# A head's outputs later in the queue of the matrix engine, and the last column's squares added up

## The chip, the cores and the metric

The kernel runs on one core of a Trainium2 chip. A core has a matrix engine (TensorE, PE in the profile, its weight loads PEld), two engines for elementwise work (VectorE, DVE; ScalarE, ACT), GpSimd (POOL) and SyncE (SP), which issues the transfers. Each engine takes its own instructions one after another, and waits where an instruction needs what another engine has not finished. The metric is the device time of one execution in microseconds.

## The reference

A trunk of two layers over 256 tokens of width 2048, in 32-bit floats. Each layer is a token mixer and a SwiGLU FFN, both behind an RMSNorm whose shift and scale come from a conditioning vector, and both added to x through a gate that comes from it too.

```python
for i in range(DEPTH):
    mod = (c_act @ w_mod[i] + b_mod[i])[:, None, :]
    sh1, sc1, g1, sh2, sc2, g2 = jnp.split(mod, 6, axis=-1)
    h = rms_norm(x, norm1_g[i]) * (1.0 + sc1) + sh1
    y = retention_mixer(h, ...) if i % 4 == 0 else short_conv_mixer(h, ...)
    x = x + g1 * y
    h = rms_norm(x, norm2_g[i]) * (1.0 + sc2) + sh2
    x = x + g2 * swiglu(h, ffn_w_in[i], ffn_w_out[i])
return rms_norm(x, final_g)
```

Layer 0 mixes by retention: eight heads, each with q and k (256 wide, rotated by position), v and a gate g (512 wide). A head's output is rms_norm(decayed causal scores of q and k, times v) times silu(g); all heads' outputs go through w_out. Layer 1 mixes by a gated convolution of width 3.

## The kernel before

**Products.** Every matrix product is made from two halves: each weight tile is rounded to a coarser format (hi, ScalarE, L413) and the rest is kept (lo, VectorE, L416), the activations likewise, and three products of halves are added up. TensorE multiplies blocks of 128 by 128. The weights lie in memory in the order of use, in chunks of 128 by 2048; a chunk makes two tiles of hi and lo, eight blocks each, and `take` hands the blocks out in order. `raw` has three buffers and hi and lo four each, so the preparation runs a few tiles ahead of TensorE. The conditioning vector's products are made on VectorE, one reduction (L327) for each of 192 chunks, spread over the kernel.

**Orders.** TensorE's order is that of the program. The order on VectorE, ScalarE and GpSimd outside the opening is made by a planner, which simulates the program with costs of its own and takes what is ready by priority. Accumulators are eight PSUM banks, given out in turn.

**Heads.** They run in the order 4, 0, 2, 1, 5, 3, 6, 7. The opening (`RET_SPANS`) computes parts of the heads 0 to 4 ahead, while the normed rows come one by one: head 4 has all 16 rows of q, k and its gate, heads 0 and 1 have 13 rows, heads 2 and 3 nine. What is made there is in `ahead`, under the head and the number of the bank: 0 for q, 1 for k, 2 and 3 for the two halves of the gate. `projections` does the rest of a head in this order: the rest of q and its rotation, the rest of k, v (16 rows of four blocks), the scores, and the rest of the gate. The head's outputs are not made there. `mixed` returns two pieces of work, `outputs` (nine matmuls of scores and v at L1055, a Square with its sum, a power on GpSimd, the product with the gate at L1064) and `turned` (eight transposes at L1074, and the split into halves), each with a number of blocks. They go to `asides`; `ticked` counts the blocks that the next work multiplies, and gives out the first piece when its number is reached, sets the count to 0, and then the second:

```python
since[0] += n
if asides and since[0] >= asides[0][0]:
    asides.pop(0)[1]()
    since[0] = 0
```

The numbers are `STEPS = (6, 26)`. The count goes up row by row: by two in q and k, by four in v, and by six in the first group of the output projection, which has six columns. That projection is done in two parts, after the fourth head (head 1) and after the eighth; a part's first group takes twelve of its sixteen rows for six columns, and then the last four rows for each of these, and all rows for each other column.

**Norms.** As a column of x is finished, `squares` adds its squares to `acc`: Square on ScalarE, addition on VectorE (L568). The first column, and before the change the last one too, goes into a tile of its own by a Square alone (L564). `norm_sums` then adds over partitions with matmuls against ones (L576), a set for each tile in the list. `normed` starts the next projection on rows that have only been scaled, does two rows, and has `norm_sums` after them; the power follows on GpSimd, and the spread of the result two rows later. `scaled_only` (L659, L660) makes each row as its column is done.

Of the kernel before, what the change touches and what calls it, by code (L numbers as in the profile page):

```python
# [48 lines left out]
STEPS = (6, 26)  # L49
# [69 lines left out]
def tiles_of(g):  # L119
    return sum(width for _, width in g.items) // P * len(g.ks)  # L120
# [147 lines left out]
def trunk(ctx: ExitStack, tc: tile.TileContext, x_in, c_in, pos_in, w_mod, cols_in, tab_in, w_all, out):  # L268
# [9 lines left out]
    def name(s):  # L278
        serial[0] += 1
        return f"{s}_{serial[0]}"  # L280

    def tmp(tag, shape=(P, S), dtype=F32, pool=work, bufs=None):
        return pool.tile(list(shape), dtype, tag=tag, name=name(tag), bufs=bufs)
# [8 lines left out]
    x = [x_all[:, j, :] for j in range(KT)]  # L292
# [52 lines left out]
    first = tiles_of(RET_SPANS[0])  # L345
# [16 lines left out]
    def needed(layer, which, last=KT - 1):  # L362
        while any(m[:2] == (layer, which) and m[2] <= last for m in todo):
            modulation(*todo.pop())
# [83 lines left out]
    def bank(tag=None):  # L448
        tag = tag or (lanes.pop(0) if lanes else lane[0])
        return ps[0].tile([P, 2, S], F32, tag=tag, name=name("bank"))  # L450
# [10 lines left out]
    def product(g, act, base=0, before=None, banks=None, last=True):  # L461

        fresh = not banks
        banks = banks or [bank() for _ in g.cols]
        if fresh and due_gap[0] <= 0:
            nc.tensor.transpose(banks[0][:, 0, :P], ident, ident)
            due_gap[0] = GAP_EVERY
        due_gap[0] -= len(g.cols) * len(g.ks)
        for k in g.ks:
            if before:  # L470
                before(k)
            h = act[k - base]
            for c, pt in zip(g.cols, banks):
                hi, lo = take(g, k, c)
                nc.tensor.matmul(  # L475
                    pt, hi, h, start=fresh and k == g.ks[0], stop=False, skip_group_check=True
                )
                nc.tensor.matmul(  # L478
                    pt[:, 1, :], lo, h[:, 0, :], start=False, stop=last and k == g.ks[-1], skip_group_check=True
                )  # L480
            ticked(len(g.cols))
        paced(len(g.cols) * len(g.ks))
        return banks

    def packed(g, act, base=0, before=None, between=None, banks=None):

        banks = banks or [bank() for _ in g.cols[::2]]
        for k in g.ks:
            if before:
                before(k)  # L490
            h = act[k - base]
            for i, c in enumerate(g.cols):
                if between and i == len(g.cols) // 2:
                    between(k)
                pt = banks[i // 2][:, i % 2, :]
                hi, lo = take(g, k, c)
                first, last = k == g.ks[0] and i % 2 == 0, k == g.ks[-1]
                nc.tensor.matmul(pt, hi, h[:, 0, :], start=first, stop=False, skip_group_check=True)  # L498
                nc.tensor.matmul(pt, hi, h[:, 1, :], start=False, stop=False, skip_group_check=True)  # L499
                nc.tensor.matmul(pt, lo, h[:, 0, :], start=False, stop=last, skip_group_check=True)  # L500
            ticked(len(g.cols))
        paced(len(g.cols) * len(g.ks))
        return banks

    def flat(pt):
        return pt.rearrange("p a b -> p (a b)")
# [54 lines left out]
    def squares(acc, t, tag="acc"):  # L561
        if acc is None:
            acc = tmp(tag, bufs=1)
            nc.scalar.activation(acc, t, AF.Square)  # L564
        else:
            sq = tmp("sq", bufs=2)
            nc.scalar.activation(sq, t, AF.Square)
            nc.vector.tensor_tensor(acc, acc, sq, op=ALU.add)  # L568
        return acc
# [142 lines left out]
    def output(groups, act, which, last, after=None, base=None):  # L712

        layer, gate = which[0], mod_g[which[0]][which[1] == GT2]
        first, *groups = groups
        due_gap[0] = 0
        base, acc = first.ks[0] if base is None else base, None
        banks = product(first, act, base, last=False)
        for j, g in enumerate(groups):
            needed(*which, j)  # L720
            col = gate[:, j : j + 1]
            if last and j == KT - 1:
                (pt,) = packed(g, act, base)
                nc.vector.scalar_tensor_tensor(x[j], pt[:, 0, :], col, x[j], op0=ALU.mult, op1=ALU.add)
                acc = [acc, squares(None, x[j], "acc1")]
                if after:
                    after(j)
                return acc
            (pt,) = product(g, act, base, banks=banks[j : j + 1])
            t = tmp("sum", bufs=4)  # L730
            nc.vector.scalar_tensor_tensor(t, pt[:, 1, :], col, x[j], op0=ALU.mult, op1=ALU.add)
            nc.vector.scalar_tensor_tensor(x[j], pt[:, 0, :], col, t, op0=ALU.mult, op1=ALU.add)
            if last:
                acc = squares(acc, x[j])
            if after:
                after(j)


    with ExitStack() as inner:
# [48 lines left out]
        ahead = {}  # L788
# [3 lines left out]
        def rm_pair(key, dtype=F32):  # L792
            tag_of[key] = free.pop(0)
            return rm.tile([P, 2, 2, S], dtype, tag=tag_of[key], name=name("rm"))
# [17 lines left out]
        with tc.tile_pool(name="start", bufs=1) as sp:  # L812
# [57 lines left out]
            with tc.manual_schedule(engines={mybir.EngineType.DVE, mybir.EngineType.Activation}):  # L870
# [24 lines left out]
                def square(i):  # L895

                    both = rm.tile([P, 2, 2, S], F32, tag=f"pair{i}", name=name("sq"))
                    sq = [both[:, n] for n in range(2)]
                    for n in range(2):
                        nc.scalar.activation(sq[n], x4[i][:, 2 * n : 2 * n + 2, :], AF.Square)  # L900
                    return sq
# [5 lines left out]
                acc = square(0)  # L907
# [136 lines left out]
        def mixed(head, both, v, sg):  # L1044

            total = tmp("rs", (P, 2), bufs=4)
            os = [rp.tile([P, DV], F32, tag="o", name=name("o"), bufs=2) for _ in range(2)]

            def outputs():
                pts = [bank() for _ in range(2)]  # L1050
                for t, pt in enumerate(pts):
                    for jt in range(t + 1):
                        a = both[jt][:, :, (t - jt) * P : (t - jt + 1) * P]
                        for x, y in ((0, 0), (0, 1), (1, 0)):
                            nc.tensor.matmul(  # L1055
                                flat(pt), a[:, x, :], v[:, jt, y, :], start=jt + x + y == 0, stop=jt == t and x == 1
                            )
                    nc.scalar.activation(os[t], flat(pt), AF.Square, accum_out=total[:, t : t + 1])
                r = tmp("rs", (P, 2), bufs=4)
                nc.vector.tensor_scalar(r, total, 1.0 / DV, EPS, op0=ALU.mult, op1=ALU.add)  # L1060
                root = tmp("rs", (P, 2), bufs=4)
                nc.gpsimd.tensor_tensor(root, r, half, op=ALU.pow)
                for t, pt in enumerate(pts):
                    nc.vector.scalar_tensor_tensor(  # L1064
                        os[t], flat(pt), root[:, t : t + 1], sg[t], op0=ALU.mult, op1=ALU.mult
                    )

            def turned():
                pts = [bank() for _ in range(2)]
                for i, pt in enumerate(pts):  # L1070
                    for j in range(2):
                        at = slice((2 * i + j) * P, (2 * i + j + 1) * P)
                        for t in range(2):
                            nc.tensor.transpose(pt[:, j, t * P : (t + 1) * P], os[t][:, at], ident)  # L1074
                for i, pt in enumerate(pts):
                    n = 2 * head + i
                    t = rm_pair(("mid", n), F32R)
                    nc.scalar.copy(t[:, :, 0, :], pt)
                    nc.vector.tensor_tensor(t[:, :, 1, :], pt, t[:, :, 0, :].bitcast(F32), op=ALU.subtract)
                    mid[2 * n], mid[2 * n + 1] = t[:, 0], t[:, 1]  # L1080

            return list(zip(STEPS, [outputs, turned]))

        def pair(head, i):

# [33 lines left out]
        acc = ret_out(1, True)  # L1119
# [29 lines left out]
    acc = swiglu(0, acc, lambda j: scaled_only(1, 0, j))  # L1149
# [4 lines left out]
    for i, g in enumerate(CONV_IN):  # L1154
        pending += [sums(g)] if i else normed(acc, 1, 0, g)
        while len(pending) >= 3:
            pb, pc, pu = pending[:3]
            pending = pending[3:]
            j = done
# [11 lines left out]
            split(mid[j], y)  # L1171
            done += 1
    acc = output(CONV_OUT, mid, (1, GT1), True, lambda j: scaled_only(1, 1, j))

    stage.close()
# [202 lines left out]
    acc = swiglu_tokens(1, acc, with_gain)  # L1378
# [48 lines left out]
```

## Time and profile before

| what | us |
|---|---|
| median of three runs | 2607.35 (2607.01 to 2611.01) |
| profiled execution | 2605.66 |
| span of its instructions | 2603.9 |
| TensorE busy in the span | 2571.1 |
| VectorE busy | 2178.4 |
| ScalarE busy | 1300.3 |

The granted clock of TensorE is 0.998 of full speed over the span. The profile lists groups of instructions by line of the program; "L1055" is line 1055, "bank<-v,sp" means that the instruction writes the tile bank and reads v and sp. In the order of time, the first number is the start in microseconds from the start of the span, the second the duration; "x9" means nine in a row, and a bracket gives the idle time of the engine before it and what ended it. In the list of waits, the numbers are the total in microseconds, the times, and the longest one.

### The profile page before, as it was taken

How to read it: one execution, taken by the hardware profiler on the slowest of the kernel's cores; microseconds unless marked ns; L12 is line 12 of the kernel's file. 1: busy time of each engine (PE TensorE's matmuls, PEld its weight loads, DVE VectorE, ACT ScalarE, POOL GpSimd, SP SyncE). 2: the span in 40 equal slices, each digit the busy share in tenths (PEclk: the TensorE clock that was granted, in tenths of full speed). 3: DMA queues.
4: the chain of work that ended last, by engine and by line, in shares of the span. 5: the costliest groups of instructions: out<-in, count | busy, mean ns of one | idle time of the engine just before them, and what ended most of it. 6: DMA issues, size and time to landing. Idle time of an engine off the chain costs nothing.

```text
span 2603.9 us, 36702 instructions
## 1 busy us (share of the span) xinstructions
PE 2571.1 (99%) x14341; PEld 2239.5 (86%) x14341; DVE 2178.4 (84%) x2751; ACT 1300.3 (50%) x1757; POOL 129.6 (5%) x230
## 2 busy tenths in 40 slices
PE   7999999999999999999999999999999999999998
PEld 5998889888889888888888898888898888888887
DVE  7998878787698887777777889888889999999984
ACT  5544543444456444334444454444565554555553
POOL 0000000120000010010000100000000000000000
PEclk9999999999999999999999999999999999999999
DMA  9976668777676887888887868877755555555553
GB/s 399 402 278 239 231 229 323 273 284 279 252 286 243 330 324 292 290 307 304 293 296 285 306 236 317 316 296 279 287 179 209 180 208 201 189 202 198 196 195 129
DMA packets 96945, 687.48 MB, mean 264 GB/s; under 512 B 10753, under 2 KB 12545, under 8 KB 13825
## 3 DMA queue, kind: packets, MB, share of 16 engines
q1 hardware_dynamic: 96194, 684.48, 71.2%
q8 instruction: 112, 1.84, 0.3%
q10 hardware_dynamic: 576, 0.66, 0.1%
q14 instruction: 63, 0.52, 0.1%
HBM read 682.99 MB, written 2.10 MB: 263 GB/s over the span
## 4 chain that ended last, share of the span: by engine, by line
PE 66%; issue 28%; DVE 3%; DMA 2%; ACT 1%; POOL 0%; SPq 0%; POOLq 0%; ACTq 0%; DVEq 0%
PE bank L475 29%; PE bank L478 15%; PE bank L514 4%; PE bank L513 4%; PE bank L515 4%; DMA raw<-w_all 2%; PE bank L499 1%; PE bank L498 1%; PE bank L500 1%; PE bank L688 1%; DVE lo L416 1%; PE bank L689 1%; PE bank L543 1%; PE bank L690 1%; PE bank L542 1%
## 5 line engine op out<-in xcount | busy, mean ns | idle before, releaser
L413 ACT CAST hi<-raw 128x1024 fp32r<-128x1024 f32 (+1 forms) x912 | 932.3, 1031 | 904.2 <-DMA raw<-w_all 268.3
L416 DVE TENSOR_TENSOR lo<-raw,hi 128x1024 fp32r<-128x1024 f32 (+1 forms) x912 | 1081.0, 1196 | 281.2 <-ACT hi L413 278.8
L475 PE MATMUL bank<-h,hi 128*128 128x512 f32 x2016 | 699.8, 391 | 0.0
L478 PE MATMUL bank<-h,lo 128*128 128x256 f32 x2016 | 564.4, 280 | 0.0
L475 PEld LDWEIGHTS bank<-h,hi 128*128 128x128 f32 x2016 | 377.0, 187 | 82.5
L327 DVE SCALAR_TENSOR_TENSOR raw<-raw,cb 128x2048 f32<-128x2048 f32 x160 | 365.8, 2286 | 33.0 <-DMA raw<-w_mod 32.6
L478 PEld LDWEIGHTS bank<-h,lo 128*128 128x128 f32 x2016 | 381.0, 189 | 0.0
L475 PE MATMUL bank<-mid,hi 128*128 128x512 f32 x922 | 321.1, 395 | 0.0
L478 PE MATMUL bank<-mid,lo 128*128 128x256 f32 x922 | 256.1, 278 | 0.3 <-DVE lo L416 0.3
L475 PEld LDWEIGHTS bank<-mid,hi 128*128 128x128 f32 x922 | 172.9, 188 | 40.5
L513 PE MATMUL bank<-hi,h 128*128 128x512 f32 x512 | 201.7, 394 | 0.0
L514 PE MATMUL bank<-lo,h 128*128 128x512 f32 x512 | 200.9, 392 | 0.1
L515 PE MATMUL bank<-hi,h 128*128 128x512 f32 x512 | 200.0, 391 | 0.0
L1187 PE MATMUL bank<-hi,h 128*128 128x512 f32 x490 | 191.5, 391 | 0.0
L1189 PE MATMUL bank<-hi,h 128*128 128x512 f32 x490 | 190.7, 389 | 0.0
L1188 PE MATMUL bank<-lo,h 128*128 128x512 f32 x490 | 190.7, 389 | 0.0
L478 PEld LDWEIGHTS bank<-mid,lo 128*128 128x128 f32 x922 | 173.3, 188 | 0.6 <-DVE lo L416 0.6
L475 PE MATMUL bank<-rm,hi 128*128 128x512 f32 x496 | 173.0, 395 | 0.0
L413 ACT CAST hi<-sums 128x1024 fp32r<-128x1024 f32 x84 | 88.4, 1052 | 143.2 <-PE bank L1189 104.0
L416 DVE TENSOR_TENSOR lo<-sums,hi 128x1024 fp32r<-128x1024 f32 x84 | 102.8, 1223 | 50.4 <-ACT hi L413 50.1
L478 PE MATMUL bank<-rm,lo 128*128 128x256 f32 x496 | 137.7, 278 | 0.0
L515 PEld LDWEIGHTS bank<-hi,h 128*128 128x128 f32 x512 | 96.6, 189 | 20.7
(230 smaller groups left out, 4098.1 us busy)
## 6 DMA issues: line engine op xcount, KB each, us to landing
raw<-w_all SPq DMA_DIRECT2D x456, 1024.0 KB, 4.9
raw<-w_mod SPq DMA_DIRECT2D x192, 1024.0 KB, 5.5
x<-x_in SPq DMA_DIRECT2D x4, 512.0 KB, 5.2
decay<-tab_in SPq DMA_DIRECT2D x8, 128.0 KB, 3.4
out<-x SPq DMA_DIRECT2D x4, 256.0 KB, 3.2
out<-x ACTq DMA_DIRECT2D x3, 128.0 KB, 2.6
out<-x SPq DMA_DIRECT2D x1, 384.0 KB, 2.6
out<-x ACTq DMA_DIRECT2D x1, 256.0 KB, 3.2
```

The source lines that it names most:

```text
L327: nc.vector.scalar_tensor_tensor(raw, raw, 1.0, cb, op0=ALU.mult, op1=ALU.mult, accum_out=total)
L413: nc.scalar.copy(hi[:, :n], raw)
L416: nc.vector.tensor_tensor(lo[:, :n], raw, hi[:, :n].bitcast(F32), op=ALU.subtract)
L475: nc.tensor.matmul(pt, hi, h, start=fresh and k == g.ks[0], stop=False, skip_group_check=True)
L478: nc.tensor.matmul(pt[:, 1, :], lo, h[:, 0, :], start=False, stop=last and k == g.ks[-1], skip_group_check=True)
L498: nc.tensor.matmul(pt, hi, h[:, 0, :], start=first, stop=False, skip_group_check=True)
L513: nc.tensor.matmul(flat(pt), a[:, 0, :], hi, start=first, stop=False)
L514: nc.tensor.matmul(flat(pt), a[:, 0, :], lo, start=False, stop=False)
L515: nc.tensor.matmul(flat(pt), a[:, 1, :], hi, start=False, stop=last)
L1187: nc.tensor.matmul(flat(pt), a[:, 0, :], hi, start=first, stop=False, skip_group_check=True)
L1188: nc.tensor.matmul(flat(pt), a[:, 0, :], lo, start=False, stop=False, skip_group_check=True)
L1189: nc.tensor.matmul(flat(pt), a[:, 1, :], hi, start=False, stop=last, skip_group_check=True)
```

## The change

In `mixed`, the number of blocks after which a head's outputs are given out becomes half of the second number, 13, where the second half of its projections' banks is in `ahead`, that is for the heads 0 to 4; for the heads 5 to 7 it stays 6. The transposes still follow 26 blocks after the outputs. In `output`, the squares of the last column are added to `acc` on VectorE, as those of the other columns, in place of going into a tile of their own; the list has one tile in place of two. This is used three times: for the second part of the retention's output projection, for that of the first layer's FFN, and for the convolution's. The second layer's FFN, ahead of the last norm, has code of its own, and keeps the tile of its own.

```diff
             if last and j == KT - 1:
                 (pt,) = packed(g, act, base)
                 nc.vector.scalar_tensor_tensor(x[j], pt[:, 0, :], col, x[j], op0=ALU.mult, op1=ALU.add)
-                acc = [acc, squares(None, x[j], "acc1")]
+                acc = [squares(acc, x[j])]
                 if after:
                     after(j)
                 return acc
...
-            return list(zip(STEPS, [outputs, turned]))
+            first = STEPS[1] // 2 if (head, 2) in ahead else STEPS[0]
+            return [(first, outputs), (STEPS[1], turned)]
```

## The prediction

> **What bounds the kernel now.** I read the page's busy times first, then the list of waits of TensorE, then the order of time around each place that the change touches.
>
> ```profile
> span 2603.9 us, 36702 instructions
> PE 2571.1 (99%) x14341; PEld 2239.5 (86%) x14341; DVE 2178.4 (84%) x2751; ACT 1300.3 (50%) x1757; POOL 129.6 (5%) x230
> ```
>
> TensorE is busy for 99% of the span, so what counts is only what it waits for and what it executes. The waits of TensorE between 200 and 2590 us, that is from the end of the opening to just before the last norm, are these four, and no more:
>
> ```profile
> PE bank L1055 <- DVE qs L1003: 2.3, 2, 1.3
> PE bank L1055 <- ACT sp L557: 0.8, 1, 0.8
> PE bank L688 <- DVE x L724: 0.7, 1, 0.7
> PE bank L478 <- DVE lo L416: 0.3, 1, 0.3
> ```
>
> L1055 are the matmuls of a head's outputs, which the first edit moves. Its two rows are the only prize of that edit. Their three places are in the work that follows head 4 and in the work that follows head 1; the other six heads show no such wait, so three of the five moved heads (0, 2 and 3) have nothing to gain.
>
> **The first edit, after head 4.** The order of time at the outputs:
>
> ```profile
> 226.32 0.28 PE L499 MATMUL bank<-h,hi 128*128 128x256 f32 x1
> 226.44 0.28 PE L500 MATMUL bank<-h,lo 128*128 128x256 f32 x1
> 227.06 0.60 ACT L557 CAST sp<-sum 128x256 fp32r<-128x256 f32 x2 [0.88 <-DVE sum L1038]
> 227.52 2.58 PE L1055 MATMUL bank<-v,sp 128*128 128x512 f32 x9 [0.80 <-ACT sp L557]
> 227.74 0.62 DVE L558 TENSOR_TENSOR sp<-sum,sp 128x256 fp32r<-128x256 f32 x2
> ```
>
> Matmuls are pipelined, so I count from start to start: a 256-wide one takes 226.44 - 226.32 = 0.12 us, the next could start at 226.56 and starts at 227.52, when the first half of the scores is rounded. That is 0.96 us lost. Head 0, the next work, has 6 blocks left of q, 6 of k, and then four blocks for each row of v. The count reaches 13 only in the first row of v (6 + 6 + 4 = 16). The ten blocks between take 3 x 0.12 = 0.36 us each: the outputs come at 226.56 + 10 x 0.36 = 230.2, while the scores are whole at 227.74 + 0.62 = 228.36. The wait goes, with 1.8 us in hand: **-0.96 us**.
>
> **The first edit, after head 1.** The next work is the first half of the output projection, whose first group counts six blocks a row, so the outputs come now after one row (6 blocks) and then after three (18).
>
> ```profile
> 339.84 0.48 PE L475 MATMUL bank<-rm,hi 128*128 128x512 f32 x1
> 341.93 0.28 PE L478 MATMUL bank<-rm,lo 128*128 128x256 f32 x1
> 342.72 0.68 DVE L1003 TENSOR_TENSOR qs<-rm,bank 128x512 f32<-128x512 f32 x1
> 343.55 0.93 PE L1055 MATMUL bank<-v,sp 128*128 128x512 f32 x3 [1.34 <-DVE qs L1003]
> 344.66 0.68 DVE L1003 TENSOR_TENSOR qs<-rm,bank 128x512 f32<-128x512 f32 x1
> 345.39 1.65 PE L1055 MATMUL bank<-v,sp 128*128 128x512 f32 x6 [0.92 <-DVE qs L1003]
> 346.88 0.39 PE L475 MATMUL bank<-rm,hi 128*128 128x512 f32 x1
> 357.48 1.03 PE L1074 MATMUL bank<-tab,o 128*128 128x128 f32 x8
> 358.73 1.29 DVE L1079 TENSOR_TENSOR rm<-bank,rm 128x512 fp32r<-128x512 f32 x2 [0.24 <-ACT rm L1078]
> ```
>
> The wait is for accumulators, not for scores: eight PSUM banks go round in the order in which they are asked for. Counted back from the outputs' two banks stand the six of the first group, and then the two that held head 1's gates, which L1003 reads. The first starts when the first read has ended (342.72 + 0.68 = 343.40), the second after the other (345.34). Lost are 343.55 - (341.93 + 0.12) = 1.50 us, and, with six 512-wide matmuls in 346.88 - 345.39 = 1.49, so 0.25 each, 345.39 - (343.55 + 0.75) = 1.09 us.
> After the change twelve more blocks lie between. A block takes (357.48 - 346.88) / 30 = 0.353 us, since the transposes stand 30 blocks behind the outputs: the outputs come at 342.05 + 12 x 0.353 = 346.3, and the second gate bank is free at 345.4. Both waits go, with 0.9 us in hand, the thinnest cover of this edit: **-2.59 us**, and 0 to -1.5 if VectorE sets the second L1003 back by one weight tile (1.2 us).
> The transposes move with them, to 18 + 30 = 48 blocks of the 72 in the first group. The rows of head 1 that they make are read only behind those 72, 24 x 0.353 = 8.5 us later; now it takes from 357.48 to 358.73 + 1.29 = 360.02, 2.5 us, until they are there. Nothing waits.
>
> **What moves, and past what.** Each head's outputs are nine matmuls, two Squares with their sums on ScalarE, L1060 and two L1064 on VectorE and one power on GpSimd between these; the transposes add eight matmuls, two casts and two subtractions. None issues a DMA, so SyncE's queue sees nothing of it. In heads 0 and 1 as next work they slip behind the rest of k and one row of v; in heads 2 and 6 by eight blocks of q (6 to 14). The work is the same, so in itself it costs 0. Its cover: v has one buffer, but the next v is written only at the end of its 16 rows, 15 rows behind; the accumulators of the outputs are asked for at most two rows later. Moved VectorE work can delay the weights' low halves; that is a rival below.
>
> **The second edit, on TensorE.** The sums of squares are made with one set of matmuls in place of two, at three norms (after the first output projection, the first FFN and the convolution; the last norm keeps its two).
>
> ```profile
> 786.24 0.95 PE L576 MATMUL bank<-ones,acc 128*128 128x1 f32 x8
> 787.05 0.37 PE L688 MATMUL bank<-h,hi 128*128 128x258 f32 x1
> ```
>
> Eight records fill 787.05 - 786.24 = 0.81 us of a TensorE that waits for nothing there. That is 0.10 us each, and half of them gives 0.41 us. If the first four covered a fixed cost of starting, it would be less, at worst nothing; I take 0.41, as L688 follows the eight without a wait. Three norms: **-1.2 us**.
> The Trainium skill, in "TensorE: Matmul & The Clock Gate", section "Wait — 56ns, not 53.3ns?", puts the shortest distance of two small matmuls at about 25 ns, however narrow; four saved would then be 0.1 us a norm, 0.3 us in all, and the sum 0.9 us later. The same page's section "LDWEIGHTS (loading the stationary operand)" gives the columns divided by 1.2, 107 ns for a load of 128, and as each of these matmuls has its own load, that would be 0.43 us a norm. The trace's 0.10 us sides with the load.
>
> **The second edit, on VectorE.** An addition joins the chain of the last column: product, Square, now the addition, then the norm's matmuls. In other columns VectorE has it directly ahead of L660:
>
> ```profile
> 763.82 0.42 DVE L568 TENSOR_TENSOR acc<-acc,sq 128x256 f32<-128x256 f32 x1
> 764.20 0.49 DVE L660 SCALAR_TENSOR_TENSOR h<-x,a,h 128x256 fp32r<-128x256 f32 x1
> ```
>
> So I put it there in the three places, 0.42 us long and taking 0.38 of the queue. The Square, VectorE around it, and the norm's matmuls:
>
> ```profile
> 782.58 0.42 ACT L564 ACTIVATE acc<-x 128x256 f32<-128x256 f32 x1 [1.83 <-DVE x L724]
> 784.67 0.48 DVE L660 SCALAR_TENSOR_TENSOR h<-x,a,h 128x256 fp32r<-128x256 f32 x1
> 785.07 2.35 DVE L416 TENSOR_TENSOR lo<-raw,hi 128x1024 fp32r<-128x1024 f32 x2
> ...
> 1520.59 2.36 DVE L416 TENSOR_TENSOR lo<-raw,hi 128x1024 fp32r<-128x1024 f32 x2 [2.15 <-ACT hi L413]
> 1521.41 0.42 ACT L564 ACTIVATE acc<-x 128x256 f32<-128x256 f32 x1
> 1522.12 0.95 PE L576 MATMUL bank<-ones,acc 128*128 128x1 f32 x8
> 1522.86 0.48 DVE L660 SCALAR_TENSOR_TENSOR h<-x,a,h 128x256 fp32r<-128x256 f32 x1
> ...
> 1878.76 0.42 ACT L564 ACTIVATE acc<-x 128x256 f32<-128x256 f32 x1
> 1880.02 0.48 DVE L660 SCALAR_TENSOR_TENSOR h<-x,a,h 128x256 fp32r<-128x256 f32 x1
> 1882.94 0.95 PE L576 MATMUL bank<-ones,acc 128*128 128x1 f32 x8
> ```
>
> First norm: the addition ends at 784.67 + 0.42 = 785.09, ahead of 786.24: 0, under cover of the two rows of the next projection that TensorE does first; behind the two L416 it would end at about 787.8 and cost 1.6. Third norm: 1880.44 against 1882.94: 0, with the same cover. Second norm: here ScalarE was held by a late weight transfer, the Square ends only at 1521.83, and VectorE is in two weight tiles until 1522.9. Ahead of L660 the addition ends at 1523.28, and the matmuls, 0.05 us behind it as in the rows above (345.34 to 345.39), start at 1523.3 in place of 1522.12: **+1.2 us**. The bounds: directly behind the Square it would end at 1522.30, +0.2; behind one more weight tile (1.2 us) +2.4. I take 1.2, from the neighbour L660. The power and the spread behind that norm wait as much later as all of TensorE.
> The wait of L688 for L724 (0.7) is for the product itself, ahead of the Square, and stays.
>
> **The sum.** -0.96 - 2.59 - 1.2 + 1.2 = **-3.6 us**. The profiled execution took 2605.66 us, of which 1.76 lie outside the span; it would be 2602.1. The median of the runs shown, 2607.35, is 1.69 above it, so I give 2603.8 on that scale. About 0.2% (5.2 us) is what a measurement of this kernel can tell from no change, and this lies inside.
>
> **The rivals.**
>
> ```profile
> 319.75 1.22 DVE L416 TENSOR_TENSOR lo<-raw,hi 128x1024 fp32r<-128x1024 f32 x1
> 322.32 0.39 PE L513 MATMUL bank<-hi,h 128*128 128x512 f32 x1
> 347.81 0.17 DVE L1060 TENSOR_SCALAR rs<-rs 128x2 f32<-128x2 f32 x1 [2.46 <-ACT o L1058]
> 348.84 1.41 DVE L1064 SCALAR_TENSOR_TENSOR o<-bank,rs,sg 128x512 f32<-128x512 f32 x2 [0.87 <-POOL rs L1062]
> ```
>
> *The addition finds a gap.* If the late transfer at the second norm comes earlier, or VectorE's order puts the addition between the two weight tiles, the 1.2 falls to 0.2 or less. Sum -4.6 to -4.75: 2602.7 (at 0.2% below, 2602.1, half of this case's spread of about 1 us lies faster). For it: VectorE idles 2.15 us right ahead of those tiles, so the late transfer alone makes the crowding. Against: nothing in the change moves that transfer.
>
> *The thin cover fails.* Head 1's gate banks stay late because VectorE's order of the gates and weight tiles shifts as well, and half of the 2.59 stays, while the addition still costs its 1.2. Sum -2.3: 2605.0; with the bound +2.4 at the second norm and the first norm's 1.6, both 2.8 more, 2607.8. For it: VectorE takes its queue in order and is 84% busy. Against: 0.9 us in hand.
>
> *Slower: VectorE is held at the moved products.* In the work after heads 0, 2 and 3 VectorE now meets L1060 and L1064 among the ropes and weight tiles of the next head. Where its queue has them ahead of TensorE's outputs, it idles as at 347.81 and 348.84: 2.46 + 0.87 = 3.3 us. In the work after head 2 the weight tile that ends at 319.75 + 1.22 = 320.97 is read at 322.32 (tiles counted in order, eight blocks each): 1.35 us of cover. A full hold costs there 3.3 - 1.35 = 2.0 us; with two more of its kind at heads 0 and 3, 6.0 us, it decides from 3.6 us, that is from two holds on. Sum -3.6 + 6.0 = +2.4: 2609.8. For it: the planner orders VectorE by its own costs. Against: the five heads' outputs come later on TensorE but later in the program too, and no weight tile is late at them now.
>
> **How the numbers follow.** Forecast 0.45, gap found 0.25, thin cover 0.18, held VectorE 0.12. The forecast's own range is 2601.5 to 2606, its terms' bounds and the scatter of the runs shown. Faster by over 0.2%: half of the second case and a quarter of the first, 0.24. Slower by over 0.2% (above 2612.6): a third of the last case and what I can't name, 0.07. Within: 0.69. For 8 in 10, the range leaves out the last case's upper half and as much below: 2600.8 to 2608.8.
>
> **What would show it.** Right: no L1055 in the list of waits for L1003 or for sp; the outputs after head 4 directly behind six-matmul rows of v; L576 with four records at three norms, and about 1.2 us of waiting for L568 at the second of them alone. Wrong: L416 as a releaser of TensorE between 225 and 600 us (held VectorE); a wait of L1055 that is left at 346 (thin cover); a wait of L576 at the first or third norm; or less than 2 us or more than 6 between the spans.

## The result, and the profile after

| | before, us | after, us |
|---|---|---|
| median of 22 runs each | 2606.49 (2603.63 to 2616.68) | 2600.76 (2598.36 to 2610.38) |
| profiled execution | 2605.66 | 2598.36 |
| its span | 2603.9 | 2596.6 |

The ratio of after to before is 0.9977, with a 95% interval of 0.997 to 0.9984: 5.73 us, or 0.22%, faster. The forecast was 2603.8 in a range of 2600.8 to 2608.8, "within 0.2%" the likeliest; the time fell at the range's lower edge, just outside it. The profiled execution of the kernel after is the fastest of its 22 runs, so the two spans lie further apart than the medians.

The page of the kernel after, its first rows, and its list of waits of TensorE between 200 and 2590 us:

```profile
span 2596.6 us, 36680 instructions
PE 2566.0 (99%) x14329; PEld 2237.0 (86%) x14329; DVE 2181.2 (84%) x2754; ACT 1299.3 (50%) x1757; POOL 133.3 (5%) x230
...
PE bank L594 <- POOL rs L587: 1.0, 1, 1.0
PE bank L576 <- ACT acc L564: 0.7, 1, 0.7
PE bank L688 <- DVE x L724: 0.7, 1, 0.7
```

TensorE has twelve matmuls fewer, four at each of three norms, and VectorE three instructions more, the three additions. No L1055 is in the list any more. The waits for L587 and L564 belong to the last norm, which comes so much earlier now that it starts inside the window. The one wait that the prediction added, of L576 for the addition at the second norm, isn't there.

The order of time of the kernel after, at the outputs of head 4 and of head 1 (start, duration, as before):

```profile
230.24 2.20 PE L1055 MATMUL bank<-v,sp 128*128 128x512 f32 x9
232.28 0.39 PE L513 MATMUL bank<-hi,h 128*128 128x512 f32 x1
...
339.83 0.68 DVE L1003 TENSOR_TENSOR qs<-rm,bank 128x512 f32<-128x512 f32 x1
341.77 0.68 DVE L1003 TENSOR_TENSOR qs<-rm,bank 128x512 f32<-128x512 f32 x1
...
345.08 2.21 PE L1055 MATMUL bank<-v,sp 128*128 128x512 f32 x9
347.13 0.39 PE L475 MATMUL bank<-rm,hi 128*128 128x512 f32 x1
```

Each head's nine matmuls now run through, in 232.28 - 230.24 = 2.04 us and 347.13 - 345.08 = 2.05 us from their start to that of the next product. The second gate bank is free at 341.77 + 0.68 = 342.45, 2.6 us ahead of the outputs.

And at the second norm, where the prediction lost 1.2 us. Rows of VectorE, ScalarE and TensorE of the kernel after, in order of time:

```profile
1513.16 0.48 DVE L724 SCALAR_TENSOR_TENSOR x<-bank,g,x 128x256 f32<-128x256 f32 x1 [0.58 <-PE bank L500]
1514.32 2.00 ACT L413 CAST hi<-raw 128x1024 fp32r<-128x1024 f32 x2 [5.23 <-DMA raw<-w_all]
1515.41 1.22 DVE L416 TENSOR_TENSOR lo<-raw,hi 128x1024 fp32r<-128x1024 f32 x1 [1.77 <-ACT hi L413]
1516.23 0.41 ACT L567 ACTIVATE sq<-x 128x256 f32<-128x256 f32 x1
1516.67 0.43 DVE L568 TENSOR_TENSOR acc<-acc,sq 128x256 f32<-128x256 f32 x1
1517.08 0.49 DVE L660 SCALAR_TENSOR_TENSOR h<-x,a,h 128x256 fp32r<-128x256 f32 x1
1517.32 0.50 PE L576 MATMUL bank<-ones,acc 128*128 128x1 f32 x4
1517.48 2.35 DVE L416 TENSOR_TENSOR lo<-raw,hi 128x1024 fp32r<-128x1024 f32 x2
1517.68 0.37 PE L688 MATMUL bank<-h,hi 128*128 128x258 f32 x1
```

The weight transfer is late here too: ScalarE can begin on the tiles only 1514.32 - 1513.16 = 1.16 us after the product L724 (1.56 us in the profile of before). But VectorE has the addition behind one weight tile, not two, and it ends at 1516.67 + 0.43 = 1517.10, 0.2 us ahead of the matmuls. The four matmuls hold TensorE for 1517.68 - 1517.32 = 0.36 us, where eight held it for 0.81.

### The profile page after: what moved, and what is told of

Same layout as the page of the kernel before. It is cut to its first block, busy times and chain, and to the rows that moved or that the text cites. A ratio compares the mean times of both kernels' runs of the same rounds, so it can differ in the third digit from the quotient of the medians.

```text
span 2596.6 us, 36680 instructions
## 1 busy us (share of the span) xinstructions
PE 2566.0 (99%) x14329; PEld 2237.0 (86%) x14329; DVE 2181.2 (84%) x2754; ACT 1299.3 (50%) x1757; POOL 133.3 (5%) x230
## 4 chain that ended last, share of the span: by engine, by line
PE 70%; issue 28%; DMA 1%; DVE 1%; ACT 0%; SPq 0%; POOL 0%; POOLq 0%; ACTq 0%; DVEq 0%
PE bank L475 30%; PE bank L478 15%; PE bank L513 4%; PE bank L514 4%; PE bank L515 4%; PE bank L498 2%; PE bank L500 2%; PE bank L499 2%; PE bank L543 1%; PE bank L542 1%; PE bank L541 1%; PE bank L688 1%; PE bank L689 1%; PE bank L690 1%; PE bank L1055 1%
## 5 line engine op out<-in xcount | busy, mean ns | idle before, releaser
L416 DVE TENSOR_TENSOR lo<-raw,hi 128x1024 fp32r<-128x1024 f32 (+1 forms) x912 | 1081.8, 1196 | 285.6 <-ACT hi L413 283.2
L475 PE MATMUL bank<-h,hi 128*128 128x512 f32 x2016 | 699.8, 391 | 0.0
L478 PE MATMUL bank<-h,lo 128*128 128x256 f32 x2016 | 564.4, 280 | 0.0
L475 PEld LDWEIGHTS bank<-h,hi 128*128 128x128 f32 x2016 | 377.0, 187 | 82.5
L478 PEld LDWEIGHTS bank<-h,lo 128*128 128x128 f32 x2016 | 381.0, 189 | 0.0
L475 PE MATMUL bank<-mid,hi 128*128 128x512 f32 x922 | 320.0, 394 | 0.0
L478 PE MATMUL bank<-mid,lo 128*128 128x256 f32 x922 | 255.4, 277 | 0.0
L475 PEld LDWEIGHTS bank<-mid,hi 128*128 128x128 f32 x922 | 172.9, 188 | 40.1
L514 PE MATMUL bank<-lo,h 128*128 128x512 f32 x512 | 200.6, 392 | 0.0
L515 PE MATMUL bank<-hi,h 128*128 128x512 f32 x512 | 199.7, 390 | 0.0
L475 PE MATMUL bank<-rm,hi 128*128 128x512 f32 x496 | 173.1, 395 | 0.0
L478 PEld LDWEIGHTS bank<-mid,lo 128*128 128x128 f32 x922 | 173.0, 188 | 0.0
L416 DVE TENSOR_TENSOR lo<-sums,hi 128x1024 fp32r<-128x1024 f32 x84 | 102.8, 1223 | 50.3 <-ACT hi L413 50.0
L478 PE MATMUL bank<-rm,lo 128*128 128x256 f32 x496 | 137.7, 278 | 0.0
L515 PEld LDWEIGHTS bank<-hi,h 128*128 128x128 f32 x512 | 96.5, 188 | 20.7
```

Of the source, the lines that this page charges most:

```text
L416: nc.vector.tensor_tensor(lo[:, :n], raw, hi[:, :n].bitcast(F32), op=ALU.subtract)
L475: nc.tensor.matmul(pt, hi, h, start=fresh and k == g.ks[0], stop=False, skip_group_check=True)
L478: nc.tensor.matmul(pt[:, 1, :], lo, h[:, 0, :], start=False, stop=last and k == g.ks[-1], skip_group_check=True)
L514: nc.tensor.matmul(flat(pt), a[:, 0, :], lo, start=False, stop=False)
L515: nc.tensor.matmul(flat(pt), a[:, 1, :], hi, start=False, stop=last)
```

## The experiments

Ratios are to the kernel before, run beside each on the same chip; its medians in the three timed sets were 2606.26, 2607.51 and 2606.67 us, and one run of it beside the kernel with head 1's outputs after four blocks took 2606.2. Differences given below are between these medians; a kernel with one run shows places and waits, not a time.

| kernel | median, us | ratio, 95% interval | profiled span, us |
|---|---|---|---|
| first edit alone | 2602.02 | 0.9984 (0.9975 to 0.9993) | 2598.9 |
| second edit alone | 2604.15 | 0.9993 (0.9984 to 1.0002) | 2601.9 |
| both | 2600.82 | 0.9978 (0.9969 to 0.9987) | 2601.6 |
| before, once more | 2607.15 | 1.0002 (0.9993 to 1.0011) | 2603.2 |
| heads 4 and 1 alone | 2602.59 | 0.9986 (0.9977 to 0.9995) | 2600.8 |
| both, addition late | 2603.64 | 0.9984 (0.9974 to 0.9993) | 2601.8 |
| both, reductions earlier | 2601.12 | 0.9984 (0.9975 to 0.9993) | 2601.5 |
| both, again | 2599.75 | 0.9974 (0.9965 to 0.9984) | 2599.2 |
| four columns in the first group | 2612.0 (one run) | | 2610.2 |
| four columns, head 1's outputs after four blocks | 2606.31 (one run) | | 2604.5 |
| both, three tiles made late | 2639.91 (one run) | | 2638.1 |

**The edits one by one.** The first:

```diff
-            return list(zip(STEPS, [outputs, turned]))
+            first = STEPS[1] // 2 if (head, 2) in ahead else STEPS[0]
+            return [(first, outputs), (STEPS[1], turned)]
```

> The first edit alone (outputs of heads 0 to 4 after 13 blocks), the norms as before. Theory W (waits): the whole gain of this edit is the waits of L1055 that it removes, 1.4 us after head 4 and 2.7 us after head 1, so the time is 4.1 us under the kernel before, no L1055 in the list of waits, and L576 keeps eight records at three norms. Rival O (order): the new order on VectorE also keeps weight tiles from being late elsewhere (0.35 us at 580 and 1.6 us around 1815 in the profile of before), and the time is 6.0 us under it. Rival P (the prediction): 3.6 us.

The second:

```diff
-                acc = [acc, squares(None, x[j], "acc1")]
+                acc = [squares(acc, x[j])]
```

> The second edit alone (last column's squares added on VectorE), outputs as before. Theory W: three norms of 0.45 us each, no wait at any of them, 1.4 us under the kernel before; the three waits of L1055 are there as before. Rival P (the prediction): 1.2 us of waiting at the second norm, so 0 to 0.2 us under the kernel before, and the list of waits names L568 for L576.

Both (the kernel after) and none (the kernel before), in the same set:

> The changed kernel once more, beside the others on this chip. Theory W: the two edits add up, 5.5 us under the kernel before. Rival O: 7.3 us, as between the two profiles. If the late weight tiles are chance, their places differ from those of the other profiles.

> The kernel before, unchanged, as a null and for a second profile of it. Theory W: the same three waits of L1055 to within 0.2 us, and the late weight tiles at 580 and 1815 us gone or elsewhere, since those came from late transfers. Rival O: these two are there again, as the order on VectorE makes them.

The first edit alone measured -4.24 us, the second alone -2.11, both -5.44, and the kernel before +0.89 against its own runs, which is how far such a median can be off; the second edit's interval alone reaches no change. The groups of instructions say more. With the first edit alone, outputs and norm matmuls (busy time and mean of one, then the idle time ahead of them):

```profile
L1055 PE MATMUL bank<-v,sp 128*128 128x512 f32 x72 | 17.7, 391 | 0.0
...
L576 PE MATMUL bank<-ones,acc 128*128 128x1 f32 x32 | 4.0, 240 | 0.7 <-ACT acc L564 0.7
```

With the second alone:

```profile
L1055 PE MATMUL bank<-v,sp 128*128 128x512 f32 x72 | 18.5, 397 | 3.4 <-DVE qs L1003 2.6 <-ACT sp L557 0.8
...
L576 PE MATMUL bank<-ones,acc 128*128 128x1 f32 x20 | 2.6, 235 | 0.7 <-ACT acc L564 0.7
```

Each edit does its own part and leaves the other's alone; the 0.7 of L576 is the last norm's, which neither touches. What the first edit is worth is read where the waits were, here in the profile of the kernel before, once more:

```profile
226.55 0.28 PE L500 MATMUL bank<-h,lo 128*128 128x256 f32 x1
227.63 2.58 PE L1055 MATMUL bank<-v,sp 128*128 128x512 f32 x9 [0.80 <-ACT sp L557]
230.05 0.28 PE L498 MATMUL bank<-h,hi 128*128 128x256 f32 x1
...
342.04 0.28 PE L478 MATMUL bank<-rm,lo 128*128 128x256 f32 x1
343.75 0.93 PE L1055 MATMUL bank<-v,sp 128*128 128x512 f32 x3 [1.42 <-DVE qs L1003]
345.59 1.65 PE L1055 MATMUL bank<-v,sp 128*128 128x512 f32 x6 [0.91 <-DVE qs L1003]
347.08 0.39 PE L475 MATMUL bank<-rm,hi 128*128 128x512 f32 x1
```

Head 4's outputs hold TensorE from 226.55 + 0.12 = 226.67 to 230.05, 3.38 us, where the kernel after takes 2.04: 1.34 saved. Head 1's hold it from 342.16 to 347.08, 4.92 us, against 2.05: 2.87 saved. Together 4.2 us. After head 4 there was a second wait, which the row of nine hides: the weight load of the third matmul waited for the second half of the scores (L558). The list of waits of the weight loads (PEld) in the profile of before, 200 to 480 us, has it:

```profile
PEld bank L1055 <- DVE sp L558: 0.4, 1, 0.4
```

As a cross-check, from the last L541, at the end of the opening, to the first L688 TensorE took 581.76 us in the profile of the kernel before, once more, and 577.63 in those of the first edit alone and of the kernel after: 4.13 us less (3.2 to 3.3 less in the two other runs of both, where one weight tile came late on the way and cost 0.8 to 0.9 from start to start). (These and the next stretches are differences of two starts in the order of time, which stand too far apart to be shown together.) Between the first and the 51st L688 lie the norm's matmuls; that stretch takes 19.44, 19.44 and 19.51 us at the three norms of the kernel before, once more, and 19.00, 18.99 and 19.06 after: 3 x 0.45 = 1.34 us for the second edit. The sum of the two edits by the traces is 5.5 us; the medians gave 5.73 and, for the two runs of both, 5.44 and 6.92.

**Heads 4 and 1 alone.** The first edit without heads 0, 2 and 3, which had no wait; the second edit left out:

```diff
-            return list(zip(STEPS, [outputs, turned]))
+            first = STEPS[1] // 2 if head in (1, 4) else STEPS[0]
+            return [(first, outputs), (STEPS[1], turned)]
```

> The first edit for the heads 4 and 1 alone; the heads 0, 2 and 3 give out their outputs after 6 blocks as before, and the norms are as before. Theory W: only these two heads had waits, so the gain is the same 4.1 us as with all five heads, and no wait of L1055 is in the list. Rival (the later products of the other three help VectorE): less than that, 3 us or below, with weight tiles late after heads 0, 2 or 3.

It measured -4.92 us (-3.7 by the ratio in the table), beside -4.24 for all five heads: the same within the scatter. The list of waits of this kernel, 200 to 2590 us:

```profile
PE bank L576 <- ACT acc L564: 0.7, 1, 0.7
PE bank L688 <- DVE x L724: 0.7, 1, 0.7
PE bank L478 <- DVE lo L416: 0.4, 1, 0.4
PE bank L514 <- DVE lo L416: 0.3, 1, 0.3
```

No L1055 is left. The other three heads give nothing, and their moved products take nothing: VectorE wasn't held there.

**The addition late.** Both edits, but the last column's addition gets a low priority, so that the planner puts it behind the weight tiles and the row L660:

```diff
-                acc = [acc, squares(None, x[j], "acc1")]
+                sq = tmp("sq", bufs=2)
+                nc.scalar.activation(sq, x[j], AF.Square)
+                with tc.high_priority(offset=MOD_PRIO):
+                    nc.vector.tensor_tensor(acc, acc, sq, op=ALU.add)
+                acc = [acc]
```

> Both edits, but the last column's addition has the low priority of the conditioning reductions, so on VectorE it stands behind L660 and the weight tiles around it: behind two tiles at the first and the second norm, behind L660 alone at the third. This is the order that the prediction assumed at the second norm. Theory C (cover): by the profile of the changed kernel the addition then ends 1.5 us behind the norm's matmuls at the first norm, 1.2 us at the second, and 2 us ahead of them at the third; TensorE waits 2.7 us in all, and the time is 2.7 us above the changed kernel, 2.8 us under the kernel before. Rival N (the wait at a norm is hidden, since the rows after it fill the time): no wait, and the time of the changed kernel.

The order of time at the first and at the second norm of this kernel (L728 is the addition):

```profile
782.63 2.36 DVE L416 TENSOR_TENSOR lo<-raw,hi 128x1024 fp32r<-128x1024 f32 x2
784.90 0.42 DVE L728 TENSOR_TENSOR acc<-acc,sq 128x256 f32<-128x256 f32 x1
785.47 0.58 PE L576 MATMUL bank<-ones,acc 128*128 128x1 f32 x4 [1.52 <-DVE cu L1167]
...
1517.78 2.36 DVE L416 TENSOR_TENSOR lo<-raw,hi 128x1024 fp32r<-128x1024 f32 x2 [0.48 <-ACT hi L413]
1520.06 0.48 DVE L660 SCALAR_TENSOR_TENSOR h<-x,a,h 128x256 fp32r<-128x256 f32 x1
1520.45 0.42 DVE L728 TENSOR_TENSOR acc<-acc,sq 128x256 f32<-128x256 f32 x1
1521.02 0.58 PE L576 MATMUL bank<-ones,acc 128*128 128x1 f32 x4
```

The kernel is 3.87 us faster than the kernel before of its set, where both edits gave 5.44 and 6.92 in theirs. The stretches over the three norms, first to 51st L688, take 20.74, 19.11 and 19.07 us, beside 19.00, 18.99 and 19.06 for the kernel after: 1.87 us more, 1.74 of it at the first norm; 2.7 was expected. At the first norm the addition stands behind two weight tiles, and TensorE waits 1.5 us; the prediction had put the price of that place at 1.6. (L1167, which the wait names, is a small memset directly behind the addition: they end at 785.32 and 785.35, and of several releasers the last is named.) At the second norm it stands behind two weight tiles as well as L660, and yet the matmuls, whose turn comes 4.17 us after L724 (1516.81 in this profile, so at 1520.98), are 0.04 us late and the stretch 0.12 longer: the transfer came earlier, VectorE started on the tiles 1517.78 - 1516.81 = 0.97 us after L724, against 2.64 in the profile of before (1520.59 - 1517.95). So where the addition stands in VectorE's order has about the price that was forecast at the first norm. At the second norm it would have it only where the transfer is late in the same execution, and no run has both. In the thirteen profiles ScalarE began on those tiles between 0.5 us before the start of L724 and 1.6 us after it, and the profile of before was the latest of them.

**Banks or data?** The wait after head 1 was put down to the accumulators. The rival: the outputs wait for the gate itself, which L1003 also reads. A smaller first group of the output projection asks for two accumulators fewer, so that the outputs get the two that come before the gate's; the gate is as it was:

```diff
-LEAD_RET, LEAD_CONV, LEAD_FFN = 6, 4, 2
+LEAD_RET, LEAD_CONV, LEAD_FFN = 4, 4, 2
```

> The kernel before, with four columns in place of six in the first group of the retention's output projection, and so two banks fewer between head 1's gates and its outputs. Theory B (banks): the outputs' two banks are then the ones of the scores, which are read earlier, and come after two rows of four, 8 blocks; the wait of L1055 for L1003 after head 1 falls from 2.6 us to 0.3 or less, and what is left names sp. Rival D (data): the outputs wait for VectorE's queue as such, the wait stays at 2 us or more and names L1003.

```profile
PE bank L478 <- DVE lo L416: 2.9, 4, 1.6
PE bank L688 <- DVE x L724: 0.9, 1, 0.9
PE bank L1055 <- ACT sp L557: 0.8, 1, 0.8
```

The wait for L1003 is gone, as the list of waits of this kernel shows, but that decided nothing: rows of four blocks let the outputs out after eight blocks in place of six, late enough for the data too. So the same was done with head 1's outputs after four blocks:

```diff
-LEAD_RET, LEAD_CONV, LEAD_FFN = 6, 4, 2
+LEAD_RET, LEAD_CONV, LEAD_FFN = 4, 4, 2
-            return list(zip(STEPS, [outputs, turned]))
+            return [(4 if head == 1 else STEPS[0], outputs), (STEPS[1], turned)]
```

> As the kernel with four columns in the first group, and head 1's outputs come after 4 blocks in place of 8, so that TensorE is there about 1.4 us earlier, before the second of head 1's gate banks has been read. Theory B (banks): the two banks are those of the scores, so the outputs start as soon as the scores are rounded and the last of the nine at the latest waits for sp; no wait of the outputs after head 1 ends with L1003. Rival D (data or queue): the fourth of the nine matmuls waits until the second L1003 has ended, with 0.05 us between, as in the kernel before.

```profile
342.19 0.69 DVE L1003 TENSOR_TENSOR qs<-rm,bank 128x512 f32<-128x512 f32 x1
343.25 2.23 PE L1055 MATMUL bank<-v,sp 128*128 128x512 f32 x9
344.40 0.68 DVE L1003 TENSOR_TENSOR qs<-rm,bank 128x512 f32<-128x512 f32 x1
345.31 0.39 PE L475 MATMUL bank<-rm,hi 128*128 128x512 f32 x1
```

That settles it: all nine matmuls run through in 345.31 - 343.25 = 2.06 us, the fourth of them starting at about 343.9 (0.23 each), while the second read of the gate ends only at 344.40 + 0.68 = 345.08; the kernel before held the last six until that read had ended. It was the bank, not the gate. (This holds for the second of the two waits. The first read of the gate had ended at 342.88, ahead of all nine, so no run takes the first wait apart.) Yet neither kernel is faster than before. With four columns the pairs of products L475 and L478 ran in a slower pattern at full granted clock (the last section) from 360 to 434 us and from 710 to 774 us, 0.353 us a pair in place of 0.347, which took back what the wait had cost: counted from the last L541 of the opening, the second of these kernels is 1.4 us ahead of the kernel before, once more, at the last L515 ahead of the projection's second part, and no longer ahead at the first L688 (581.78 us, beside 581.76).

**Late weight tiles.** The profile of before shows a weight tile that came late at 1815 us and slower products behind it. Is it the late tile that makes them slow? Both edits, and three tiles far apart in which VectorE's subtraction is done eight times over (extra work with the same outcome):

```diff
-        nc.vector.tensor_tensor(lo[:, :n], raw, hi[:, :n].bitcast(F32), op=ALU.subtract)
+        for _ in range(8 if prepared[0] in (331, 401, 641) else 1):
+            nc.vector.tensor_tensor(lo[:, :n], raw, hi[:, :n].bitcast(F32), op=ALU.subtract)
```

> The changed kernel, with the low half of three weight tiles (about 990, 1190 and 1850 us) made eight times over on VectorE, so that each is some 8.5 us late; the values are the same. Each makes TensorE wait, by 2 to 3 us beyond its cover of 6. Theory K (cadence): after a wait the pairs of L475 and L478 can go on at 353 ns in place of 347, as in the profile of before from 1815 to 1877 us, until the next transposes; at one of the three places or more, that adds 0.7 us (39 us to the next transposes), 2 us (110 us) or 0.4 us. Rival: the pairs keep 347 ns everywhere, and only the waits are added.

The order of time at the first of the three (the edit adds a line, so L478 and L416 are L479 and L417 here), and the busy times of the engines in a window behind it (PE, PEld, DVE, ACT, POOL, then the granted clock, the DMA share and GB/s):

```profile
996.51 0.58 PE L479 MATMUL bank<-h,lo 128*128 128x256 f32 x1 [10.88 <-DVE lo L417]
...
996.60:1002.00 5.40, 5.40 (x18) 4.64 (x19) 1.67 (x1) 0.56 (x1) 0.20 (x2) 0.52 0.95 372
```

The size was wrong by far: waits of 11, 7 and 9 us came out where 2 to 3 were meant, and with such waits the clock is another cause, so the run doesn't answer its question cleanly. Behind each of the three waits TensorE ran at half the granted clock for 5.2 to 5.3 us (the window shown, 5.4 us long, has 0.52 as its mean), which the short waits told of above never brought. After that, at full clock, the slower pattern followed the first of these waits, until the next transposes at 1038 us, and not the other two. It also ran from 1414 to 1530 us and from 1708 to 1810, each time from directly behind transposes (L466 in the kernel before) and with no wait of TensorE there. So a late tile isn't needed for it.

**The late tile at 1815.** Does the load on VectorE make it? Both edits, and the reductions of the conditioning vector spread so that they end earlier:

```diff
-    plan_mod = [(early, 0), (1024, 18), (1984, 49), (5152, n_mod)]
+    plan_mod = [(early, 0), (1024, 18), (1984, 49), (4928, n_mod)]
```

> Both edits, and the conditioning reductions are spread so that all of them are done when the convolution's output projection begins (the last point of their plan is 4928 blocks in place of 5152). Theory L (late tile): the weight tile that is late around 1812 us, in kernels with and without the edits, is late because two chunks for reductions stand ahead of it among the transfers and two reductions (2.29 us each) ahead of it on VectorE; without these it is in time, the wait of 0.5 to 1.2 us and the slower pairs behind it (up to 1.1 us) go, and the time is 0.7 to 2 us under the changed kernel. Rival M: the reductions, closer together, make tiles late elsewhere, and the time is the changed kernel's or above.

Both edits once more in the same set:

> The changed kernel a third time, beside the one with earlier reductions. Theory W: 5.5 us under the kernel before; a wait of 0.5 to 1.2 us for a weight tile around 1812 us in this profile too, in either pair cadence after it.

With the reductions earlier, nothing is late at 1815. One tile is at 1070 instead:

```profile
1070.80 0.38 PE L478 MATMUL bank<-mid,lo 128*128 128x256 f32 x1 [0.77 <-DVE lo L416]
```

Both edits without it, in the same set, have one tile 0.5 us late at 463 us (L514) and one 0.6 late at 1811 (L478).

So in this one profile the lateness moved with the reductions but wasn't saved, and 2601.12 beside 2599.75 us is no gain: no version here beats the kernel after. In the other twelve profiles a tile is late at that place in eleven (near 1815 us, or later where longer waits stand ahead of it); that of the kernel after is the exception.

## Why the prediction was right and where it failed

The direction and the places where time is saved were right, one wait was forecast that did not come, and the size was too small: 5.5 us by the traces, where the sum said 3.6. By its own steps:

- **Head 4's outputs, -0.96.** The wait went, and 1.34 was saved. The missing 0.38 is the nine matmuls themselves: 2.42 us (227.63 to 230.05) directly behind the wait, 2.04 when nothing is late. The forecast counted only the gap ahead of the first of them, though its own row had 2.58 us for nine, and the second half of the scores was still being made as they ran: the third weight load waited for it (L558). In the profile of the kernel before, once more, the first four starts are 0.33, 0.37 and 0.33 us apart, and the later ones 0.23 to 0.24.
- **Head 1's outputs, -2.59.** Both waits went, and 2.87 was saved. The three and the six were taken at 0.75 and 1.49 us, 2.24 together, where nine undisturbed ones take 2.05: behind each wait the second matmul starts some 0.1 us later than it would in a free row. And the first wait was 0.1 longer in the second profile of the same kernel. That the second wait was for its bank is shown by the second four-column kernel; for the first it is argued. The thin cover, 0.9 us, was 2.6.
- **Three norms, -1.2.** They saved 0.45 each, 1.34. Half of eight was the right rule, and a trifle low: the 0.81 us of eight and the 0.36 of four differ by 0.45 for four, 0.11 each. The Trainium skill, in "TensorE: Matmul & The Clock Gate", section "LDWEIGHTS (loading the stationary operand)", gives the columns divided by 1.2, by estimate 107 ns for a load of 128, and the trace agrees; the 25 ns of the section "Wait — 56ns, not 53.3ns?" isn't what these matmuls cost.
- **The wait at the second norm, +1.2: this step failed.** It took the neighbour L660 as it stood before, behind two weight tiles, and assumed that the addition would come directly ahead of it there. The planner put the addition and L660 between the two tiles instead. It is the second edit that brings this place: with the first edit alone L660 stays behind both tiles, with the second alone the addition and L660 stand between them. With that order even the Square of the profile of before, which ends at 1521.83, gives an addition that ends at about 1522.3, 0.2 us behind the matmuls' turn at 1522.12: the bound that the prediction gave for "directly behind the Square", and did not take. So 1.0 of the 1.2 was the order, and the rest a lateness of one transfer that was 0.4 us smaller in the profile after and differs from run to run. The late addition bears out the price of a place behind two tiles at the first norm (1.5 us of waiting, 1.7 over the stretch, where 1.6 was said). In the kernel with reductions earlier the planner did put the addition behind two tiles and ahead of L660 at the second norm, as the prediction had it. VectorE began on the tiles 0.6 us after L724 there, the addition ended at 1520.77, and L576 started at 1521.64 without a wait. So the forecast order cost nothing there, where the transfer wasn't late. Why the planner chose the place can't be read from a trace; that the extra 0.4 us on VectorE's queue changed what was ready when it chose is argued, not shown.
- **The baseline.** The forecast added 1.69 us from the profiled execution to the median of three runs; over 22 runs that median is 2606.49, 0.86 lower.

The miss of 3.04 us is thus 1.2 for the failed step, 0.8 for the three terms that were too small (0.38 + 0.28 + 0.14), 0.86 for the baseline, and 0.2 that the scatter covers.

Of the rivals, "the addition finds a gap" came true as a mechanism, by the second of the two ways it named; its 2602.7 was still too slow by the terms above. "The thin cover fails" and "VectorE is held at the moved products" did not happen: no L1055 waits, and no L416 releases TensorE between 225 and 600 us in the profile after. (In the two other runs of both one tile was late, 0.6 us at 465 and 0.5 at 463, more than 100 us behind the last moved products; ScalarE had waited for its transfer. The profile of before had one that was 0.3 late at 580.) One of the prediction's own signs of error did show, more than 6 us between the spans (2603.9 - 2596.6 = 7.3). The edits account for 5.5; the rest is in the profile of before, which had a tile late at 580 us (0.3), one at 1815 (0.5), and slower products behind that one for some 56 us (about 1.0), and in that of after, which had no late tile at all. Against the second profile of the kernel before, with 2603.2, it is 6.6.

## What to carry to other kernels

Where matmuls wait, price the stretch from the last undisturbed start to the next undisturbed start, and compare it with the same instructions running freely: the gap ahead of the first of them is a lower bound. Where a planner makes an engine's order, a neighbour's old place is no evidence of a new instruction's place; take both sides of it as the bounds of the term. With the reductions spread otherwise, the same planner took the other side. A cost that rests on one transfer being late in one profile should be weighed by how late it is in others.

## What the runs showed of the hardware that was not expected

**Two patterns at one clock.** The pairs of products L475 and L478 run in one of two steady patterns, at a granted clock of 1.00 in both. The same pairs in the profile of before and in that of the kernel before, once more, first and last of eight:

```profile
1849.65 0.40 PE L475 MATMUL bank<-mid,hi 128*128 128x512 f32 x1
...
1852.12 0.40 PE L475 MATMUL bank<-mid,hi 128*128 128x512 f32 x1
```

```profile
1849.65 0.39 PE L475 MATMUL bank<-mid,hi 128*128 128x512 f32 x1
...
1852.08 0.39 PE L475 MATMUL bank<-mid,hi 128*128 128x512 f32 x1
```

Seven pairs take 2.47 us in the one and 2.43 in the other, 0.353 and 0.347 us a pair over longer stretches. It is the same program; both had the tile late at 1815, and only in one did the slower pattern follow, to the end of that run of pairs at 1871 us. Of nine profiles with this tile late by 0.3 to 1.0 us (not counting the first four-column kernel and the one with tiles made late), it followed in three: the profile of before and the two other runs of both. The latest tile, 1.0 us with the second edit alone, did not bring it. The kernels with four columns, with tiles made late and with reductions earlier also went into it directly behind transposes, without a wait: the last of them from 1393 to 1509 us. It ended at transposes (1025 us there, 1038 and 1810 in the kernel with tiles made late), once at a wait of 0.3 us (1747 in the first four-column kernel), else with its run of pairs. So a wait or transposes can start it or end it, and need not; what sets it stays open.

**The clock after a wait.** Behind the opening, waits of 0.3 to 1.6 us never lowered the granted clock. Behind the waits of 10.9, 7.0 and 9.0 us in the kernel with tiles made late it was 0.5 for 5.2 to 5.3 us. But the opening of each of the thirteen profiles has a stretch of 3.41 us at half clock as well, behind a wait of 1.8 to 2.4 us, here in the profile of before (the second row has the columns of the window shown above):

```profile
49.68 0.39 PE L543 MATMUL bank<-h,lo 128*128 128x256 f32 x1 [2.23 <-DVE lo L416]
...
50.03:53.44 3.41, 3.41 (x15) 3.02 (x14) 3.03 (x3) 2.03 (x3) 0.00 (x0) 0.50 1.01 420
```

Not every such wait brings it: 2.10 us at 41.6 us in the same profile did not. The Trainium skill, in "TensorE: Matmul & The Clock Gate", section "What's actually happening", states half the clock after at least one idle window of about 3.4 us, and full clock after at least one such window of busy time, where the windows run on their own and don't start with the work. The trace agrees with the half, and 3.4 and 5.2 us are one window and between one and two; but here the half clock came behind waits of some 2 us too, which are shorter than a window.
